# Two-layer diffusion trunk on one core: context products of gate and up made beside the sample products, activation sums kept in SBUF, modulation rows computed by halves

## The chip, the cores and the metric

One core of a Trainium2 chip runs the whole program. Its engines are TensorE (PE, with its weight loads as PEld), VectorE (DVE), ScalarE (ACT) and GpSimd (POOL); SyncE (SP) and POOL issue the DMAs that this text speaks of. The metric is the device time of one execution in microseconds (us), as the median of several runs.

## The reference

Two layers run over 256 context tokens and 1024 sample tokens (1280 columns in all, model width 1024, 8 blocks of 128). A layer has a modulated RMS norm, a projection into a pooling branch, a differential attention branch and a gating branch, an output projection, and a SwiGLU feed-forward part. The change lies in the second half:

```
m = silu(cond) @ w_ada + b_ada          -> sh1, sc1, g1, sh2, sc2, g2
x  = x + g1 * (y @ w_out)
h2 = rms_norm(x, norm2_g) * (1 + sc2) + sh2
gate, up = split(h2 @ w_ffn_in)         # 2 x 2816 columns
x  = x + g2 * ((silu(gate) * up) @ w_ffn_out)
```

The context and the sample use the same weights, with different conditioning vectors. D_FF = 2816 is 22 blocks of 128; the letter f counts them.

## The kernel before

Activations are held transposed (model width on the partitions, tokens along the free axis) in three chunks: c = 0 is the context (256 columns), c = 1 and c = 2 are the halves of the sample (512 columns each). All operands of matmuls are split into a rounded part and a remainder (`split`, L104: a copy on ACT at L105, a subtraction on DVE at L106), and each product takes three matmuls (`mm3`, L194, matmuls at L199). A weight slab is 128 x 1024 (512 KB): it is loaded by SP into a raw buffer and split into one of four buffers `w`.

The feed-forward input of a layer has two stages.

- The context stage: for each of the 22 f, the gate slab and the up slab are loaded and split, and two groups of 24 matmuls of 256 columns are made (`ctx_gate`, `ctx_up`). Into this loop are put the modulation of sample half c = 2 (`mod_keep`, f = 4 to 7) and, at f = 9, 11, 13 and 15, `act_sums`: four sums of activation blocks, made by POOL from modulated activations that had been written to DRAM (`HS`) and are read back into `q` (L1156), and then split.
- The sample stage: gate and up of both sample halves are a 2 x 2 block product. It is made with seven block products instead of eight (`seven`, products at L1200, each 12 matmuls of 512 columns), from sums of weight blocks (`sums`, POOL at L145 to L148) and the sums of activations. Both slabs of each f are loaded again here, into four raw buffers `raws` that take the place of the context activations. One call of `seven` for one f is called a seven below.

In layer 0, 64 rows of the modulation (`ada_row`, L246: a 128 x 1024 block of w_ada by SP into the raw ring of two, four multiply-and-reduce instructions on DVE at L255, each followed by the reading of its accumulator) are computed beside this: 8 during the output projection, and 56 during the seven products. The other 16 of layer 0 come earlier.

PE's order is the order in which the code is written. On the other engines a scheduler places the instructions when the program is built, as early as its own model of the buffers and the engines allows; each engine then runs its instructions in that order, and an instruction that waits holds up those behind it.

Of the kernel before, what the change touches and what calls it, by code (L numbers as in the profile page):

```python
# [38 lines left out]
SWAP = [(i + 16) % 32 for i in range(32)]  # L39

# [6 lines left out]
def build(tc, d):  # L47
# [45 lines left out]
    HS = [dr.tile([2, KD, P, 512], F32, name=f"HS{l}") for l in range(DEPTH)]  # L93
# [17 lines left out]
    def slab(src, extra=False):  # L111
        if extra:
            raw = pools["rx"].tile([P, 1024], F32, tag="rx", bufs=2, name=nm("raw"))
            nc.sync.dma_start(raw, src)
        else:
            raw = raw_slab(src)
        w = wp.tile([P, 2, 1024], F32R, tag="w", bufs=4, name=nm("w"))
        split(w[:, 0], w[:, 1], raw)
        ready.append(w)

    def sums(l, f):
        raws = []
        last = f == NF - 1

        def load(i):
            raw = wp.tile([P, 1024], F32, tag="raw", bufs=2, name=nm("raw")) if last else pools["raw"]()
            nc.sync.dma_start(raw, d["w_fi"][l, f, i])
            raws.append(raw)  # L130
            return raw

        def split_w(raw):
            w = wp.tile([P, 2, 1024], F32R, tag="w", bufs=4, name=nm("w"))
            split(w[:, 0], w[:, 1], raw)
            return w

        def second():
            u, g = load(1), raws[0]
            if last:  # L140
                wh = split_w(u)
            else:
                wh = pools["wh"].tile([P, 2, 512], F32R, tag="wh", bufs=2, name=nm("wh"))
                split(wh[:, 0], wh[:, 1], u[:, 512:])
# [4 lines left out]
            ready.append(wh if last else (split_w(g), wh))  # L149

        queue.extend([lambda: ready.append(split_w(load(0))), second])
        if last:
            queue.append(lambda: ready.append(split_w(raws[0])))
        queue.append(lambda: ready.append(split_w(raws[1])))

    def want(l):
        def add(src, *extra):
            queue.append(lambda: slab(src, *extra))
# [14 lines left out]
        for f in range(NF - 1):  # L173
            for i in range(2):
                add(d["w_fi"][l, f, i], f > 1 and f % 2 == 1)
        sums(l, NF - 1)
        for f in range(NF - 1):
            sums(l, f)
# [69 lines left out]
    def ada_row(l, j, condb):  # L248
        wt = raw_slab(d["w_adaT"][l, j])
# [19 lines left out]
    class Norm:  # L269
# [56 lines left out]
        def mod_keep(self, k, h, l, Ag, sh0, pair=True):  # L326
            q = COND[self.c]
            t = self.tmp()
            V.scalar_tensor_tensor(t, in0=self.x[:, k], scalar=Ag[l][:, k, q:q + 1], in1=self.rb,
                                   op0=ALU.mult, op1=ALU.mult)  # L330
            sh = mods[l][:, sh0 + k, q:q + 1]
            if pair:
                S.activation(h[:, 0, k], t, AF.Identity, bias=sh)
                V.scalar_tensor_tensor(h[:, 1, k], in0=t, scalar=sh, in1=h[:, 0, k].bitcast(F32),
                                       op0=ALU.add, op1=ALU.subtract)
            S.activation(self.x[:, k], t, AF.Identity, bias=sh)
# [179 lines left out]
    for l in range(DEPTH):  # L516
# [546 lines left out]
        prep = opened(pre, "pre")

        def spill(c):
            t0, n = CH[c]
            nc.gpsimd.dma_start(XS[:, t0:t0 + n].rearrange("(k p) t -> p k t", p=P), xs[c])

        for c in (1, 2):
            for m in range(4):  # L1070
# [3 lines left out]
                ada_next(1)  # L1074
        ws = load_w(4)
        ns = norms(prep, xs, 1)
        h2 = act_tiles("h2")

        def mod_c(c, k):
            ns[c].mod_keep(k, h2[c], l, A2, 3 * KD, c == 1 or k >= 4)  # L1080
            if k >= 4:
                nc.gpsimd.dma_start(HS[l][c - 1, k - 4::4].rearrange("k p t -> p k t"), xs[c][:, k - 4::4])

        order = [k for j in range(4) for k in (j, j + 4)]
        for c in range(3):
# [25 lines left out]
            spill(c)  # L1111
# [28 lines left out]
        tq = ExitStack()  # L1140
        tt = {}


        hq = ExitStack()

        def act_sums(j):
            if j == 0:
                pre.close()
                xq.close()
                for i in (3, 4):  # L1150
                    tt[i] = opened(tq, "tq", side="right").tile([P, 2, 4, 512], F32R, name=nm("T"))
                tt[2] = opened(fa, "t2").tile([P, 2, 4, 512], F32R, name=nm("T"))
                tt["q"] = opened(hq, "hq")
            q = tt["q"].tile([P, 2, 2, 512], F32, tag="q", bufs=1, name=nm("q"))
            for c in range(2):
                nc.sync.dma_start(q[:, c], HS[l][c, j::4].rearrange("k p t -> p k t"))  # L1156
            b11, b21, b12, b22 = q[:, 0, 0], q[:, 0, 1], q[:, 1, 0], q[:, 1, 1]
            G.tensor_sub(b11, b12, b11)
            G.tensor_sub(b12, b22, b12)
            G.tensor_sub(b22, b22, b11)  # L1160
            G.tensor_sub(b21, b21, b22)
            for t, src in ((h2[2], b11), (tt[3], b12), (tt[2], b22), (tt[4], b21)):
                split(t[:, 0, j], t[:, 1, j], src)
            if j == 3:
                hq.close()
                pools["wh"] = opened(fa, "wh")

        for f in range(NF):
            w = load_w(2)
            ctx_up(w[1], f, ctx_gate(w[0]))  # L1170
            if f == 2:
                ns[2].stat()
            if f == 4:
                ns[2].rows()
            if 4 <= f < 8:
                for k in order[2 * f - 8:2 * f - 6]:
                    mod_c(2, k)
            if 9 <= f < 16 and f % 2:
                act_sums((f - 9) // 2)
        raws = actp.tile([P, 4, 1024], F32, tag="act0", name=nm("raws"))  # L1180
        turn = [0]

        def next_raw():
            turn[0] += 1
            return raws[:, turn[0] % 4]

        pools["raw"] = next_raw
# [17 lines left out]
        t1, t2, t3, t4 = part(h2[2], 0), part(tt[2], 0), part(tt[3], 0), part(tt[4], 0)  # L1205
# [254 lines left out]
```

## Time and profile before

| | us |
|---|---|
| median of 3 runs | 3116.3 (3113.7 to 3119.6) |
| profiled execution, own time | 3117.8 |
| its span, first to last instruction | 3116.0 |
| layer 0: output projection, context stage, sample stage | 536 to 648, 648 to 800, 800 to 1281 |
| layer 1: context stage, sample stage | 2208.4 to 2359.8, 2359.8 to 2789.5 |

The stage times are from the span's start. In the span PE has matmuls under way for 2935.4 us, DVE is busy for 2046.8, ACT for 1170.7 and POOL for 619.2. In a group of instructions the first number after the bar is the time in which any of them ran, the second the mean length of one in ns, and behind the second bar stands the engine's idle time just before them, with what ended it.

### The profile page before, as it was taken

To read this page: it belongs to the slowest core of one execution; us is meant where nothing else is said; L and a number is where in the kernel's file an instruction comes from. 1 tells how busy PE (TensorE), PEld (TensorE's weight loads), DVE (VectorE), ACT (ScalarE), POOL (GpSimd) and SP (SyncE) were. 2 spreads that over 40 slices of the span, in tenths; PEclk is the share of its full clock that TensorE was granted. 3 is DMA by queue.
4 is the path that set the end of the run, shared out by engine and by line. 5 is a ranking of instruction groups with operands and counts; after the bars stand their busy time and mean duration, and the time that the engine had idled before them with its cause. 6 is when DMAs were issued, how large, how long until landed. Compare 5 with 4: busy or idle time off the path is not lost.

```text
span 3116.0 us, 41585 instructions
## 1 busy us (share of the span) xinstructions
PE 2935.4 (94%) x15800; PEld 2511.3 (81%) x15800; DVE 2046.8 (66%) x3221; ACT 1170.7 (38%) x1945; POOL 619.2 (20%) x703
## 2 busy tenths in 40 slices
PE   7999899998888899999989999999989999999997
PEld 5888788888776678888877887888888888888886
DVE  6876787676799954777684467873763444448777
ACT  4423676264222233311152236761643333322112
POOL 1222200023332333000021222000133333320002
PEclk9999999999999999999999999999999999999999
DMA  6576533366444431622123565331663222233221
GB/s 222 163 223 184 166 98 121 109 233 215 159 148 161 166 108 68 213 92 76 60 102 95 168 173 170 99 108 54 222 223 106 82 81 83 86 140 132 76 77 68
DMA packets 157815, 415.25 MB, mean 133 GB/s; under 512 B 19888, under 2 KB 51888, under 8 KB 157360
## 3 DMA queue, kind: packets, MB, share of 16 engines
q1 hardware_dynamic: 112608, 305.46, 30.4%
q0 software_dynamic: 44720, 106.98, 10.2%
q8 instruction: 124, 2.03, 0.3%
q14 instruction: 75, 0.61, 0.1%
q10 hardware_dynamic: 288, 0.16, 0.0%
HBM read 313.43 MB, written 99.09 MB: 132 GB/s over the span
## 4 chain that ended last, share of the span: by engine, by line
PE 66%; DVE 13%; DMA 8%; issue 6%; ACT 4%; POOL 2%; SPq 0%; DVEq 0%; POOLq 0%; ACTq 0%
PE f L199 26%; PE f L1200 19%; PE pa L199 7%; DVE ps L255 4%; PE pa L431 4%; PE S L371 4%; DMA raw<-w_adaT 4%; PE ps L389 3%; DVE w L106 2%; PE ps L904 2%; DMA kb<-KS 1%; DMA q<-HS 1%; DVE stt L375 1%; ACT E L378 1%; ACT w L105 1%
## 5 line engine op out<-in xcount | busy, mean ns | idle before, releaser
L199 PE MATMUL f<-ft,w 128*128 128x512 f32 (+1 forms) x3168 | 613.1, 356 | 0.7 <-DVE x L1027 0.7
L199 PEld LDWEIGHTS f<-ft,w 128*128 128x128 f32 x3168 | 523.1, 189 | 87.3 <-DVE x L1027 1.1
L1200 PE MATMUL f<-h,w 128*128 128x512 f32 x2112 | 505.8, 392 | 17.4 <-DVE pc L1230 9.4
L1027 DVE SCALAR_TENSOR_TENSOR x<-f,mod,x 128x512 f32<-128x512 f32 (+1 forms) x576 | 364.1, 658 | 221.9 <-PE f L199 220.7
L1200 PEld LDWEIGHTS f<-h,w 128*128 128x128 f32 x2112 | 396.6, 188 | 108.7 <-DVE pc L1230 14.8
L105 ACT CAST w<-raw 128x1024 fp32r<-128x1024 f32 x190 | 195.7, 1048 | 530.9 <-PE f L199 424.5
L106 DVE TENSOR_TENSOR w<-raw,w 128x1024 fp32r<-128x1024 f32 x190 | 233.8, 1245 | 113.1 <-ACT w L105 112.7
L199 PE MATMUL f<-h,w 128*128 128x256 f32 x2112 | 268.6, 291 | 34.0 <-DVE w L106 34.0
L199 PEld LDWEIGHTS f<-h,w 128*128 128x128 f32 x2112 | 265.2, 199 | 36.8 <-DVE w L106 36.7
L1200 PE MATMUL f<-T,w 128*128 128x512 f32 x1080 | 264.8, 394 | 2.3 <-ACT pc L1123 2.3
L199 PE MATMUL pa<-h,w 128*128 128x512 f32 (+1 forms) x1296 | 249.2, 353 | 0.8 <-DVE vn L607 0.8
L1200 PEld LDWEIGHTS f<-T,w 128*128 128x128 f32 x1080 | 203.8, 189 | 48.1 <-ACT pc L1123 2.7
L199 PEld LDWEIGHTS pa<-h,w 128*128 128x128 f32 x1296 | 212.3, 192 | 32.3 <-DVE vn L607 1.0
L375 DVE TENSOR_REDUCE stt<-S 128x1 f32<-128x1280 f32 x128 | 189.8, 1486 | 70.5 <-PE S L371 70.5
L431 PE MATMUL pa<-w,h 128*128 128x512 f32 x912 | 221.3, 401 | 9.5 <-DVE w L106 8.9
L199 PE MATMUL f<-mix,w 128*128 128x512 f32 (+1 forms) x1152 | 224.8, 355 | 0.0
L105 ACT CAST w<-raws 128x1024 fp32r<-128x1024 f32 x126 | 132.4, 1051 | 235.1 <-PE f L1200 196.2
L106 DVE TENSOR_TENSOR w<-raws,w 128x1024 fp32r<-128x1024 f32 x126 | 172.7, 1371 | 70.9 <-ACT w L105 70.9
L431 PEld LDWEIGHTS pa<-w,h 128*128 128x128 f32 x912 | 174.0, 193 | 50.6 <-DVE w L106 6.9
L199 PEld LDWEIGHTS f<-mix,w 128*128 128x128 f32 x1152 | 190.1, 189 | 29.5
L371 PE MATMUL S<-kb,aq 128*128 128x512 f32 (+1 forms) x768 | 196.7, 381 | 17.9 <-DMA kb<-KS 11.1
L1116 POOL DMA_DIRECT2D FS<-sg x132 | 72.6, 550 | 676.1 <-DVE sg L1232 511.0
(216 smaller groups left out, 3824.2 us busy)
## 6 DMA issues: line engine op xcount, KB each, us to landing
raw<-w_fi SPq DMA_DIRECT2D x88, 512.0 KB, 4.8
raws<-w_fi SPq DMA_DIRECT2D x84, 512.0 KB, 3.5
raw<-w_adaT SPq DMA_DIRECT2D x80, 512.0 KB, 3.9
ft<-FS SPq DMA_DIRECT2D x44, 640.0 KB, 5.1
FS<-sg POOLq DMA_DIRECT2D x88, 256.0 KB, 2.3
raw<-w_fo SPq DMA_DIRECT2D x44, 512.0 KB, 5.4
kb<-KS SPq DMA_DIRECT2D x64, 320.0 KB, 6.4
raw<-w_in SPq DMA_DIRECT2D x20, 512.0 KB, 3.8
```

Of the source, the lines that this page charges most:

```text
L105: S.copy(hi, src)
L106: V.tensor_sub(lo, src, hi.bitcast(F32))
L199: PE.matmul(ps, lhsT=a, rhs=b, start=(i == 0), stop=(i == n - 1))
L255: V.tensor_tensor_reduce(out=junk, in0=wt[:, u * 512:(u + 1) * 512], in1=condb[:, q, u * 512:(u + 1) * 512], scale=1.0, scalar=acc, op0=AL ...
L371: PE.matmul(ps[:, o:o + n], lhsT=aq[:, m, q0:q0 + P], rhs=kb[m][1 - p][:, o:o + n], start=(p == 0), stop=(p == 1))
L375: V.reduce_max(st[:, m:m + 1], ps[:, :nkey], axis=AX.X, negate=True)
L389: PE.matmul(o[:, :P], lhsT=pt[:, i * P:(i + 1) * P], rhs=vt(b + i), start=(b + i == 0), stop=(b + i == nk - 1))
L431: PE.matmul(ps, lhsT=a[:, y], rhs=wk[:, z], start=(k == 0 and x == 0), stop=(k == KD - 1 and x == 2))
L904: PE.transpose(T_["tp", b][:, x * P:(x + 1) * P], T_["E"][0][:, (4 * b + x) * P:(4 * b + x + 1) * P], ident)
L1027: V.scalar_tensor_tensor(xs[c][:, m], in0=ps, scalar=mods[l][:, g0 + m, COND[c]:COND[c] + 1], in1=xs[c][:, m], op0=ALU.mult, op1=ALU.add)
L1116: nc.gpsimd.dma_start(FS[l][f, :, t0:t0 + n], sg)
L1200: PE.matmul(ps, lhsT=y, rhs=z, start=(first and i == 0), stop=(i == 11), skip_group_check=not first)
```

## The change

- The context loop runs over f = 0 to 7 alone. For f = 8 to 21 the context's gate group is made inside `seven`, from the same split gate slab as the sample's, and the up group from the two split halves of the up slab (A21 and A22). For f = 0 to 6 both slabs are still loaded a second time; f = 7 is the first seven and uses the slabs of the last context step.
- `sums` makes the weight sums in another order with five POOL instructions for four, and splits A21 too (in every seven but the first). Raw slabs go round the ring of two and one further buffer `rx`.
- The sample activations live in four tiles `xg` (one for blocks k and k + 4 of both halves). They are modulated in place, `act_sums` reads them there, and its results T go into the same room; HS and q from DRAM are gone. `act_sums` runs at f = 2, 3, 4 and 5, right behind the modulation of c = 2.
- In the feed-forward part the modulation is computed by half rows (`ada_half`): 256 KB into two buffers `ra` of its own, two reductions each, with half of the conditioning vector in `condh`, which is loaded again when the other half begins. 8 rows belong to the output projection as before, 56 rows (112 halves) to the rest.
- The old `x` is written to XS in parts, and the squares for the norms go through two buffers.

```diff
+FIRST = 8
...
     def sums(l, f, i, first=False):
...
+                raws.append(wraw(d["w_fi"][l, f, 1], i + 1))
+                a22 = half(raws[1][:, 512:])
+            g, u = raws
             G.tensor_add(u[:, 512:], u[:, :512], u[:, 512:])
-            G.tensor_sub(u[:, :512], g[:, :512], u[:, :512])
             G.tensor_sub(g[:, :512], u[:, 512:], g[:, :512])
             G.tensor_sub(g[:, 512:], g[:, 512:], g[:, :512])
...
+            if first:
+                ready.append(split_w(g))
+            else:
+                ready.append(half(u[:, :512]))
+            G.tensor_sub(u[:, :512], u[:, 512:], u[:, :512])
+            G.tensor_sub(u[:, :512], u[:, :512], g[:, :512])
+            ready.append(split_w(u))
...
+    def ada_half(l, j, u, pool, first):
+        wt = pool.tile([P, 512], F32, tag="ra", bufs=2, name=nm("ra"))
+        nc.sync.dma_start(wt, d["w_adaT"][l, j, :, u * 512:(u + 1) * 512])
+        junk = psum()
+        for q in range(2):
+            o = mods[l][:, j, q:q + 1]
+            V.tensor_tensor_reduce(
+                out=junk, in0=wt, in1=pools["condh"][:, q], scale=1.0,
...
+        def mod_keep(self, k, l, Ag, sh0, h=None):
+            q, x = COND[self.c], self.x[:, k]
+            V.scalar_tensor_tensor(x, in0=x, scalar=Ag[l][:, k, q:q + 1], in1=self.rb, op0=ALU.mult, op1=ALU.mult)
+            S.activation(x, x, AF.Identity, bias=mods[l][:, sh0 + k, q:q + 1])
+            if h is not None:
+                split(h[:, 0, k], h[:, 1, k], x)
...
-            for c in range(2):
-                nc.sync.dma_start(q[:, c], HS[l][c, j::4].rearrange("k p t -> p k t"))
...
+            G.tensor_sub(q1, b12, b11)
+            G.tensor_sub(q3, b22, b12)
+            V.tensor_sub(q2, b22, q1)
+            G.tensor_sub(q4, b21, q2)
...
-        for f in range(NF):
+        for f in range(FIRST):
...
+            ada_halves(4 if f > 5 else 0)
+            if 2 <= f < 6:
+                for k in order[2 * f - 4:2 * f - 2]:
                     mod_c(2, k)
+                act_sums(f - 2)
...
+            if ctx:
+                pg = ctx_gate(wg)
+                ada_halves(2)
+            a21, s31 = (None, rest) if first else rest()
...
+            ada_halves(2)
+            if ctx:
+                ctx_up((a21, wh), f, pg)
```

On PE, in the sample stage, one seven stood alone. This is one of layer 0 before: f names the PSUM banks, h and T the activations, w and wh the split weights.

```order
L1200 MATMUL f_7757<-h_969_5414,w_7687 128x512 x12
L1200 MATMUL f_7692<-T_6622,w_7669 128x512 x12
L1200 MATMUL f_7784<-h_968_5413,w_7618 128x512 x12
L1200 MATMUL f_7692<-T_6614,w_7687 128x512 x12
L1200 MATMUL f_7828<-h_968_5413,w_7754 128x512 x12
L1200 MATMUL f_7692<-T_6618,wh_7662 128x512 x12
L1200 MATMUL f_7757<-h_969_5414,w_7669 128x512 x12
```

In the changed kernel PE's place from the middle of one seven with context to the middle of the next reads thus (L214 with h_987 are the context's matmuls of 256 columns).

```order
L1247 MATMUL f_7822<-h_988_5443,w_7819 128x512 x12
L1247 MATMUL f_7644<-T_6139,wh_7686 128x512 x3
L1247 MATMUL f_7644<-T_6222,wh_7686 128x512 x3
L1247 MATMUL f_7644<-T_6305,wh_7686 128x512 x3
L1247 MATMUL f_7644<-T_6388,wh_7686 128x512 x3
L214 MATMUL f_7862<-h_987_5442,wh_7782 128x256 x12
L214 MATMUL f_7862<-h_987_5442,wh_7686 128x256 x12
L1247 MATMUL f_7790<-h_989_5444,w_7692 128x512 x12
L1247 MATMUL f_7822<-T_6132,w_7899 128x512 x12
L1247 MATMUL f_7938<-h_988_5443,w_7819 128x512 x12
L214 MATMUL f_7954<-h_987_5442,w_7819 128x256 x24
L1247 MATMUL f_7997<-h_989_5444,w_7994 128x512 x12
```

The context's up group (from the halves wh_7782 and wh_7686) and its gate group (from the same w_7819 as the sample's) now stand between the seven products.

On DVE, in the context stage of layer 0, two context steps stood between one `act_sums` and the next: L106 is the remainder of a split, L1137 the product of gate and up.

```order
L106 TENSOR_TENSOR w_6643<-raw_6641,w_6643 128x1024
L1137 TENSOR_TENSOR sg_6603<-sg_6603,f_6578 128x256
L106 TENSOR_TENSOR w_6648<-raw_6646,w_6648 128x1024
L106 TENSOR_TENSOR w_6707<-raw_6705,w_6707 128x1024
L106 TENSOR_TENSOR h_969_5414<-q_6769,h_969_5414 128x512
L1137 TENSOR_TENSOR sg_6701<-sg_6701,f_6676 128x256
L106 TENSOR_TENSOR T_6614<-q_6769,T_6614 128x512
L106 TENSOR_TENSOR T_6622<-q_6769,T_6622 128x512
L106 TENSOR_TENSOR w_6712<-raw_6710,w_6712 128x1024
L106 TENSOR_TENSOR T_6618<-q_6769,T_6618 128x512
```

In the changed kernel DVE has in the same stage, for one step (L356 is the modulation, L1217 a sum, L1200 the product of gate and up):

```order
L356 SCALAR_TENSOR_TENSOR xg_4897<-xg_4897,A_0_87,ps_6116 128x512 x2
L106 TENSOR_TENSOR w_6233<-raw_6231,w_6233 128x1024
L106 TENSOR_TENSOR w_6238<-raw_6236,w_6238 128x1024
L1217 TENSOR_TENSOR q_6134<-xg_4897,q_6133 128x512
L106 TENSOR_TENSOR h_989_5444<-xg_4897,h_989_5444 128x512
L106 TENSOR_TENSOR h_989_5444<-q_6133,h_989_5444 128x512
L106 TENSOR_TENSOR T_6132<-q_6134,T_6132 128x512
L106 TENSOR_TENSOR T_6222<-q_6133,T_6222 128x512
L106 TENSOR_TENSOR T_6222<-q_6134,T_6222 128x512
L1200 TENSOR_TENSOR sg_6291<-sg_6291,f_6266 128x256
```

The modulation, all five small splits and one sum now stand together in each of four steps that follow each other, with two slab splits in the midst of them.

On DVE, in the sample stage of layer 0, a piece of a seven before (the ISA lines are a reduction and the reading of its accumulator):

```order
L1232 TENSOR_TENSOR sg_8087<-sg_8087,f_7971 128x512
L106 TENSOR_TENSOR wh_8220<-raws_7458,wh_8220 128x512
L255 ISA ps_8714,mod_84<-raw_8712,condb_5115,mod_84 128x512
L255 ISA mod_84 128x1
L1238 TENSOR_TENSOR sg_8149<-pc_8061,f_8036 128x512
L255 ISA ps_8721,mod_84<-raw_8719,condb_5115,cols 128x512
L255 ISA mod_84 128x1
L106 TENSOR_TENSOR w_8176<-raws_7458,w_8176 128x1024
L1240 TENSOR_TENSOR sg_8149<-sg_8149,pc_8105 128x512
```

And in the changed kernel:

```order
L1279 TENSOR_TENSOR pc_7065<-pc_7065,f_7040 128x512
L283 ISA ps_7676,mod_84<-ra_7674,condh_5303,cols 128x512
L283 ISA mod_84 128x1
L106 TENSOR_TENSOR w_7180<-raw_7112,w_7180 128x1024
L106 TENSOR_TENSOR wh_7257<-raw_7255,wh_7257 128x512
L283 ISA ps_7676,mod_84<-ra_7674,condh_5303,cols 128x512
L283 ISA mod_84 128x1
L283 ISA ps_7681,mod_84<-ra_7679,condh_5303,cols 128x512
L283 ISA mod_84 128x1
L283 ISA ps_7681,mod_84<-ra_7679,condh_5303,cols 128x512
L283 ISA mod_84 128x1
L1281 TENSOR_TENSOR sg_7029<-sg_7029,f_6929 128x512
```

Before, each of 13 sevens of layer 0 had 16 reductions but the last of them; now each of the first eight has 12 to 15 (mostly 14), each of the next five 20, all five with context products, and the last nine 2 in all. The splits of S31 (w_7180) and of the halves stand among them.

## Rows read from the trace of the kernel before

**Rows 1.** The page: busy time by engine, and the chain by engine.
```profile
PE 2935.4 (94%) x15800; PEld 2511.3 (81%) x15800; DVE 2046.8 (66%) x3221; ACT 1170.7 (38%) x1945; POOL 619.2 (20%) x703
PE 66%; DVE 13%; DMA 8%; issue 6%; ACT 4%; POOL 2%; SPq 0%; DVEq 0%; POOLq 0%; ACTq 0%
```

**Rows 2.** Table by stretch: busy us and count per engine, PE clock, DMA share, GB/s.
```profile
536.00:648.00 112.00, 112.00 (x594) 96.52 (x594) 76.73 (x173) 34.84 (x55) 12.50 (x13) 1.00 0.36 120
648.00:800.00 152.00, 134.82 (x1066) 133.61 (x1065) 95.58 (x112) 78.87 (x111) 47.00 (x50) 0.96 0.62 215
800.00:1281.00 481.00, 439.49 (x1851) 351.31 (x1851) 358.93 (x630) 144.06 (x198) 151.43 (x129) 0.98 0.41 137
849.48:1082.20 232.72, 205.19 (x840) 161.34 (x840) 215.98 (x413) 64.83 (x90) 74.75 (x60) 0.96 0.48 158
2208.40:2359.80 151.40, 134.54 (x1065) 133.12 (x1064) 97.85 (x112) 78.16 (x111) 47.16 (x51) 0.95 0.63 216
2359.80:2789.50 429.70, 425.75 (x1851) 348.06 (x1850) 176.58 (x199) 143.98 (x198) 140.12 (x129) 1.00 0.26 88
2402.60:2614.40 211.80, 211.80 (x926) 173.52 (x925) 86.19 (x99) 71.46 (x99) 71.83 (x66) 1.00 0.24 82
```

**Rows 3.** PE in order of time, context stage of layer 0: start, us, what.
```profile
683.49 34.79 PE L199 MATMUL f<-h,w 128*128 128x256 f32 x288
```

**Rows 4.** Groups on DVE from 2402.6 to 2614.4, layer 1: one of several.
```profile
L1224 DVE TENSOR_TENSOR sg<-pc,f 128x512 f32<-128x512 f32 x11 | 7.6, 687 | 55.1 <-PE f L1200 55.1
```

**Rows 5.** Groups on DVE from 849.48 to 1082.20, layer 0.
```profile
L255 DVE CUSTOM_DVE_ANT_0 ps<-raw,condb,cols 128x512 f32<-128x512 f32 x81 | 71.2, 888 | 16.0 <-DMA raw<-w_adaT 16.0
L106 DVE TENSOR_TENSOR w<-raws,w 128x1024 fp32r<-128x1024 f32 x30 | 46.3, 1544 | 0.0
L1224 DVE TENSOR_TENSOR sg<-pc,f 128x512 f32<-128x512 f32 x10 | 6.8, 683 | 0.0
```

**Rows 6.** DVE and POOL in order of time, inside one seven of layer 0.
```profile
1018.54 2.30 DVE L106 TENSOR_TENSOR w<-raws,w 128x1024 fp32r<-128x1024 f32 x1
1021.36 1.78 DVE L255 CUSTOM_DVE_ANT_0 ps<-raw,condb,mod 128x512 f32<-128x512 f32 x1
...
1024.78 0.75 DVE L255 CUSTOM_DVE_ANT_0 ps<-raw,condb,cols 128x512 f32<-128x512 f32 x1
...
1020.98 1.60 POOL L147 TENSOR_TENSOR raws<-raws 128x512 f32<-128x512 f32 x1 [1.23 <-DVE w L106]
```

**Rows 7.** Waits from 648 to 800: us in total, times, longest.
```profile
POOL q L1158 <- DMA q<-HS: 23.7, 4, 9.0
PE f L199 <- DVE w L106: 17.2, 6, 4.5
```

**Rows 8.** Groups on DVE and ACT from 648 to 800, context stage of layer 0.
```profile
L106 DVE TENSOR_TENSOR w<-raw,w 128x1024 fp32r<-128x1024 f32 x43 | 51.9, 1221 | 29.2 <-ACT w L105 29.2
L106 DVE TENSOR_TENSOR T<-q,T 128x512 fp32r<-128x512 f32 x12 | 13.9, 1165 | 0.7
L1137 DVE TENSOR_TENSOR sg<-sg,f 128x256 f32<-128x256 f32 x21 | 8.7, 415 | 5.2 <-PE f L199 5.0
L329 DVE SCALAR_TENSOR_TENSOR nt<-x,A,ps 128x512 f32<-128x512 f32 x12 | 8.7, 742 | 0.0
L105 ACT CAST w<-raw 128x1024 fp32r<-128x1024 f32 x43 | 44.2, 1042 | 25.9 <-PE f L199 11.4 <-DMA raw<-w_fi 6.7 <-POOL raw L148 5.2
L336 ACT ACTIVATE x<-nt,mod 128x512 f32<-128x512 f32 x14 | 9.9, 714 | 0.7 <-DVE nt L329 0.6
L105 ACT CAST T<-q 128x512 fp32r<-128x512 f32 x12 | 7.4, 620 | 9.9 <-POOL q L1160 4.3 <-POOL q L1159 3.5 <-POOL q L1161 1.9
```

**Rows 9.** DMA issues, KB each, median us to landing: 849 to 1082, and 648 to 800 (last).
```profile
raw<-w_adaT SPq DMA_DIRECT2D x40, 512.0 KB, 3.7
FS<-sg POOLq DMA_DIRECT2D x20, 256.0 KB, 2.7
raw<-w_fi SPq DMA_DIRECT2D x37, 512.0 KB, 5.0
```

More of the change, by code (lines that the diff above doesn't have):

```diff
@@ L109, in build, with wtile, wraw @@
     pools = {}
-    def slab(src, extra=False):
-        if extra:
-            raw = pools["rx"].tile([P, 1024], F32, tag="rx", bufs=2, name=nm("raw"))
-            nc.sync.dma_start(raw, src)
-        else:
-            raw = raw_slab(src)
-        w = wp.tile([P, 2, 1024], F32R, tag="w", bufs=4, name=nm("w"))
+    def wtile():
+        return wp.tile([P, 2, 1024], F32R, tag="w", bufs=4, name=nm("w"))
+    def wraw(src, i):
+        if i % 3 == 2 and "rx" in pools:
+            raw = pools["rx"].tile([P, 1024], F32, tag="rx", name=nm("raw"))
+            nc.sync.dma_start(raw, src)
+            return raw
+        return raw_slab(src)
@@ L118, in slab, with sums @@
+    def slab(src, i=0):
+        raw = wraw(src, i)
+        w = wtile()
         split(w[:, 0], w[:, 1], raw)
         ready.append(w)
-    def sums(l, f):
+        return raw
+    def sums(l, f, i, first=False):
         raws = []
[L125 to L131, printed above, removed]
@@ L133, in split_w, with half @@
         def split_w(raw):
-            w = wp.tile([P, 2, 1024], F32R, tag="w", bufs=4, name=nm("w"))
+            w = wtile()
             split(w[:, 0], w[:, 1], raw)
             return w
[L138 to L141, printed above, removed]
-            else:
-                wh = pools["wh"].tile([P, 2, 512], F32R, tag="wh", bufs=2, name=nm("wh"))
-                split(wh[:, 0], wh[:, 1], u[:, 512:])
+        def half(raw):
+            w = pools["wh"].tile([P, 2, 512], F32R, tag="wh", bufs=3, name=nm("wh"))
+            split(w[:, 0], w[:, 1], raw)
+            return w
@@ L148, in second, with rest @@
             G.tensor_sub(g[:, 512:], g[:, 512:], g[:, :512])
[L149 to L154, printed above, removed]
+            if not first:
+                ready.append((split_w(g), a22))
+        def rest():
+            g, u = raws
+            if first:
+                ready.append(split_w(g))
[4 more added lines that the diff above has]
+            ready.append(split_w(u))
@@ L156, in want, with add @@
+        queue.extend([gate, up, rest])
     def want(l):
-        def add(src, *extra):
-            queue.append(lambda: slab(src, *extra))
+        def add(src, *i):
+            queue.append(lambda: slab(src, *i))
         for j in range(4):
@@ L172, in want @@
             add(d["w_out"][l, m])
-        for f in range(NF - 1):
+        for f in range(FIRST - 1):
             for i in range(2):
[L175 to L178, printed above, removed]
+                add(d["w_fi"][l, f, i], 2 * f + i if f > 1 else 0)
+        sums(l, FIRST - 1, 2 * FIRST - 2, True)
+        for i, f in enumerate([*range(FIRST - 1), *range(FIRST, NF)]):
+            sums(l, f, 2 * (FIRST + i))
         for f in range(NF):
@@ L248, in ada_row @@
     def ada_row(l, j, condb):
[L249 removed]
+        raw = raw_slab(d["w_adaT"][l, j])
+        wt = [raw[:, :512], raw[:, 512:]]
         junk = psum()
@@ L1158, in act_sums @@
[L1158 to L1166, printed above, removed]
-        for f in range(NF):
+                tt["q"] = [pools["wh"].tile([P, 2, 512], F32, tag="wh", bufs=3, name=nm("q")) for _ in range(2)]
@@ L1210, in product1, with seven @@
             return wg, ps, copied(ps)
-        def seven(f, wg, pa_, p1, s24, wh, s31, more, first):
-            if not first:
-                fetch(1)
-            pc = fpsum(512)
-            product(pc, quarter(s31, 1), t1)
+        def seven(f, wg, pa_, p1, s24, wh, rest, more, ctx):
+            first = not callable(rest)
             product(pa_, quarter(s24, 0), t2, False)
```

154 lines of the change are left out of this document (87 added, 67 removed).

## The prediction

> **What bounds the kernel now.** I read the share of busy time first: TensorE (PE) is busy for 94 % of the span and carries 66 % of the chain, DVE 13 % and DMA 8 % [rows 1]. No matmul is removed by this change, so it can win only idle time of PE, and only in the stages that it touches. The table by stretch gives that. During the output projection (536 to 648) PE is busy for all 112.0 us, so nothing is lost there. The context stages take 152.0 us (layer 0) and 151.4 (layer 1), the sample stages 481.0 and 429.7 [rows 2], together 1214.1.
>
> What would PE alone need? In one unbroken run of the context stage 288 matmuls, 12 groups of 24, take 34.79 us [rows 3]: 2.90 a group, 5.80 for gate and up of one f, 127.6 for 22 f. In layer 1, 11 sevens take 211.80 us with PE busy throughout [rows 2]: 19.25 each, 423.6 for 22. The losses are then 24.4 and 23.8 in the context stages, 57.4 and 6.1 in the sample stages, 111.7 in all. That is the most the change can win.
>
> Who causes each? In the sevens of layer 1 DVE waits for PE (55.1 us over 11 sevens [rows 4]): PE is the bound. In layer 0 it is the other way: between 849.48 and 1082.20 ten sevens take 23.27 each, with DVE busy for 215.98 of 232.72 us [rows 2] and most of its remaining time waiting for the w_ada row (16.0 us [rows 5]). So a seven there lasts 21.60 of DVE work and 1.6 of waits. PE's granted clock is 0.96 there, near its upper level of 2.4 GHz, against 1.00 in layer 1 [rows 2]; that costs nothing of its own while PE waits. In the context stage PE waits 17.2 us for the remainders of slabs on DVE, and POOL 23.7 us for activations read back from DRAM [rows 7], with which the sums and their splits come late in DVE's order.
>
> **The context stage after.** The DRAM round trip and its 23.7 us go. What is late next is DVE itself, because modulation and sums of c = 2 now stand in four steps that follow each other. From the first modulation to the split that the first seven needs, DVE has 8 modulations of 0.74, 10 slab remainders of 1.22 [rows 8], 24 small remainders and subtractions of 0.68 (by the row of 0.683 for the same tile size [rows 5]) and 5 products of half that size, 0.42 by estimate: 5.9 + 12.2 + 16.3 + 2.1 = 36.5. Small remainders took 1.165 beside POOL before [rows 8]; 12 POOL operations now stand among them, and I stretch DVE by 0.69 for each: 8.2, in sum 44.7. In the same time PE has six f and half a group more, 6 x 5.80 + 2.7 = 37.5. So PE loses 7.2 in layer 1, and in layer 0, with 4 reductions more among them (2.7), 9.9. At the stage's start ACT's casts and modulations (1.042, 0.620 and 0.714 each [rows 8]) take about as long as PE's first groups; I charge 4 there and 2 for the first group itself. In layer 0 eight reductions and small splits stand behind the first S31 and before the next gate slab, some 9 us against the 5.5 that PE has at hand: 4. Sum: 20 in layer 0 and 13 in layer 1, each give or take 12.
>
> **Context with the sevens.** For 14 f in each layer the slabs are loaded once: 14 x 2 slab splits go in each layer, 28 x 1.22 = 34 us of DVE and 28 x 1.04 = 29 of ACT. PE's own work is the same 5.80 beside 19.25, so 25.05 for a seven with context. PE waited for little there in layer 1, and DVE has about 5 us to spare in each [rows 4]; the extra half split (0.68 on DVE, one POOL operation of 1.6) fits in. I charge 3 for layer 1's sevens.
>
> **Layer 0's sevens.** DVE's work has to be taken apart. Of the 21.60, 3 slab splits cost 3.66, six of 0.68 cost 4.1 and a stretch beside POOL some 3.1: a reduction takes 1.78 where POOL runs against 0.75 where it doesn't, a slab split 2.30 [rows 6] against 1.22. In ten sevens there are 30 such instructions, three to the four POOL sums. With 0.1 of others, 16 reductions are left at 0.665 each, their accumulator reads with them. After, each of the eight sevens without context has mostly 14 reductions, 3 slab splits, 7 small ones and five POOL sums: 9.31 + 3.66 + 4.76 + 4.12 = 21.85 (four stretches of 1.03), with 0.8 of waits 22.6. PE needs 19.25; the loss is 3.4, seven times (the first has its slabs): 23.8. Five sevens with context have 20 reductions and one more product: 13.30 + 3.66 + 4.76 + 0.42 + 4.12 = 26.26, with 1.4 of waits 27.7 against 25.05, so 2.6 x 5 = 13; of this I take off 6, as slabs lie split ahead by about one seven. The last nine have 2 reductions in all: no loss. Reloading the half conditioning vector in mid-sevens holds the reductions up once: 2.
>
> The waits for half rows are not shown by the trace. A whole row of 512 KB lands in 3.7 us, a 256 KB transfer on POOL's queue in 2.7 [rows 9], and the order leaves about 2 us between the release of a buffer and the reduction that wants it next, at some three places. So 0 to 3 us a seven, over 13 sevens from -12 to +24 around what I took; my value stands by the 2.7 row. The stretch is 3 to 5 a seven, another -14 to +12. In the output projection the eight rows are as many as before beside a PE that waits for nothing, and DVE is busy 76.73 of 112 us [rows 2]; cost 0, and 4 if the shorter transfers expose it.
>
> **A rule against this change.** In the trace a POOL sum of 1.60 lengthens a DVE instruction by about 1.03, three times in four, 0.77 per sum [rows 6]. The Trainium skill, "SBUF — State Buffer", section "Who interferes with whom", says that a DVE instruction with two SBUF inputs contends with a GpSimd instruction that reads SBUF, and that whoever issues second is blocked for the whole of it. By this rule the five sums would cost a seven 8.0 instead of 4.1; the trace bears it out only in part, so it stands below as a rival.
>
> **Sum.** Losses after: 20 + 13 + 23.8 + 7 + 2 + 3 = 68.8, against 111.7: a gain of 42.9. The profiled execution took 3117.8 (its span 3116.0, and 1.8 outside); 3117.8 - 42.9 = 3074.9. It lies 1.5 above the median of the runs, 3116.3; less that 3073.4, said as 3074.
>
> **The rivals.** *DVE's lag is not felt.* Slabs are split up to one seven ahead, and the last nine sevens have DVE nearly free, so PE might work off a reserve; the loss would be 30 (the two starts, and half of layer 0's first eight sevens), the time 3117.8 - 81.7 - 1.5 = 3035. For it: in layer 1 DVE waits for PE all along [rows 4]. Against: in layer 0 as it is, ten sevens in a row have no reserve [rows 5], and the new order still has eight in which DVE's work is above PE's. Chance 0.15.
>
> *The raw ring.* Three raw slots serve a seven where four did, and two of its sums work in place before the slots come free. A slab lands 5.0 us after its issue under load [rows 9]. If some 1.5 us of that shows in each seven, layer 1 loses 22 x 1.5 = 33 and the time is about 3107. For it: both slabs are read by POOL until late in the seven. Against: the order has each slab ready 6 us and more before it is wanted. Chance 0.12.
>
> *Slower: POOL and DVE exclude each other fully.* Each of the five sums then costs DVE its own 1.6: 8.0 - 4.1 = 3.9 more in each of 13 sevens of layer 0, 51; the 24 operations of the activation sums cost 0.91 more each where PE waits for DVE, 22. In layer 1's sevens DVE's spare time hides it. That makes 3074 + 73 = 3147. It turns from gain to loss where a POOL operation costs DVE 42.9 / 89 = 0.48 more than the 0.8 that I took, 1.3 us each. For it: the operations now stand close together, and there are more of them. Against: the measured 0.77. Chance 0.08. That the context products don't fit where they were put, and the second loads stay, is excluded by the order.
>
> **Chances and range.** My forecast has 0.65. Its own range is 3055 to 3095 (terms of ±12 in two stages, ±20 for waits and stretch, partly cancelling). The range for 8 in 10 reaches to both neighbours: 3040 to 3107. A change of 0.2 %, 6 us, is about what a measurement here can tell. Faster than that: the forecast, the first rival and the ring in most of its range, 0.84; the same 0.08, from the ring's upper end and a part of the exclusion; slower 0.08.
>
> **What would show it.** Per step: PE idle from the stage's start to the first seven's end 20 and 13 us, waiting for DVE's remainders, with no wait for DRAM left; the first eight sevens of layer 0 at 22 to 23 us and the five behind them at about 27, DVE busy throughout; the last nine and layer 1's at 25.05 with PE unbroken, 19.25 without context. I am wrong if PE waits in layer 1's sevens (the ring), if the first sevens of layer 0 come at 19 to 20 (the reserve), or if DVE's instructions beside POOL are all longer by 1.6 (exclusion).

## The result and the profile after

The changed kernel takes 3130.8 us (median of 8 runs, 3129.2 to 3148.1) against 3117.0 of the kernel before (8 runs): a ratio of 1.0055, 95 % interval 1.0038 to 1.0073. It is slower by half a percent. 3074 had been forecast, in a range of 3040 to 3107.

The page's busy time and chain of the changed kernel, beside [rows 1]:

```profile
PE 2940.2 (94%) x15800; PEld 2511.3 (80%) x15800; DVE 2034.7 (65%) x3215; ACT 1139.9 (36%) x1933; POOL 669.1 (21%) x737
PE 69%; DVE 13%; DMA 7%; issue 4%; ACT 4%; POOL 2%; SPq 0%; DVEq 0%; POOLq 0%; ACTq 0%
```

The page hardly shows a difference. The table by stretch does: layer 0's context stage, its eight sevens without context, the six sevens with context that have reductions, and the last eight; then layer 1's context stage and all its sevens (columns as in [rows 2]).

```profile
646.01:712.44 66.43, 52.04 (x394) 50.76 (x392) 60.63 (x77) 42.60 (x65) 29.54 (x22) 0.93 0.33 108
712.44:908.90 196.46, 167.82 (x673) 130.82 (x672) 178.91 (x300) 56.86 (x81) 75.21 (x60) 0.95 0.44 139
908.90:1094.50 185.60, 160.54 (x769) 132.37 (x770) 158.60 (x292) 42.36 (x66) 53.26 (x46) 0.95 0.42 133
1094.50:1299.75 205.25, 203.83 (x1083) 175.46 (x1082) 73.05 (x92) 62.82 (x89) 61.64 (x63) 1.00 0.25 84
2225.91:2293.08 67.17, 53.65 (x394) 52.45 (x393) 59.25 (x72) 42.45 (x65) 28.57 (x23) 0.90 0.33 106
2293.08:2800.25 507.17, 505.26 (x2523) 427.67 (x2523) 195.90 (x235) 164.86 (x235) 173.05 (x166) 1.00 0.23 78
```

With PE's prices (5.80 for an f of context, 19.25 for a seven) the losses are:

| stretch | before | forecast | after |
|---|---|---|---|
| layer 0, context stage | 24.4 (22 f) | 20 | 66.4 - 46.4 = 20.0 (8 f) |
| layer 0, sevens without context | | 23.8 | 196.5 - 8 x 19.25 = 42.4 |
| layer 0, sevens with context and reductions | | 7 + 2 | 185.6 - 6 x 25.05 + 2.9 = 38.2 |
| layer 0, last eight | | 0 | 1.9 |
| layer 0, all sevens | 57.4 | 32.8 | 82.5 |
| layer 1, context stage | 23.8 | 13 | 67.2 - 46.4 = 20.8 |
| layer 1, sevens | 6.1 | 3 | 2.4 |
| sum | 111.7 | 68.8 | 125.7 |

(The 2.9 is half an f of context: the first of those six makes the gate group alone, and the last of the 22 the odd up group.) PE loses 14.0 more than before; the medians lie 13.8 apart, the profiled executions 12.7 (3130.5 and 3117.8). Layer 1 wins 6.7, layer 0's context stage 4.4; layer 0's sevens lose 25.1 more, and every seven without context took 24.1 to 25.5 us there, where the kernel before took 23.27 [rows 2].

Where does a seven's time go? This is the stretch from 736.7 to 908.9, seven sevens without context (columns as above), with two of DVE's groups, and what PE and ACT wait for there (us in total, times, longest):

```profile
736.70:908.90 172.20, 146.36 (x589) 114.03 (x588) 157.60 (x264) 48.75 (x70) 62.55 (x50) 0.95 0.44 141
L283 DVE CUSTOM_DVE_ANT_0 ps<-ra,condh,cols 128x512 f32<-128x512 f32 x96 | 101.8, 1091 | 14.0 <-DMA ra<-w_adaT 13.4
L106 DVE TENSOR_TENSOR w<-raw,w 128x1024 fp32r<-128x1024 f32 x23 | 28.6, 1244 | 0.6 <-ACT w L105 0.6
```
```profile
ACT sg L1291 <- DVE sg L1290: 43.0, 7, 7.8
PE f L1247 <- ACT pc L1182: 23.2, 13, 2.5
```

PE waits for ACT's copy of a PSUM bank, ACT stands behind an activation that waits for DVE, and DVE is busy (157.6 us) or waiting (14.6, of which 13.4 for half rows) all the time. A reduction takes 1.091 in the mean; 0.753 where no POOL sum runs (third experiment). The time by which an instruction lasts longer than undisturbed is called a hold-up below. For the reductions it is 96 x 0.338 = 32.4 us; summed over all DVE instructions that took over 0.2 longer, it is 33.9, or 4.8 in a seven. Before, it was 3.2. The waits are 2.0 a seven, before 1.6 [rows 5].

One encounter of a POOL sum with reductions in order of time, and a sum that met no DVE instruction:

```profile
788.88 0.75 DVE L283 CUSTOM_DVE_ANT_0 ps<-ra,condh,cols 128x512 f32<-128x512 f32 x1
789.10 1.67 POOL L153 TENSOR_TENSOR raw<-raw 128x512 f32<-128x512 f32 x1 [11.15 <-DVE wh L106]
...
789.55 1.78 DVE L283 CUSTOM_DVE_ANT_0 ps<-ra,condh,cols 128x512 f32<-128x512 f32 x1
...
793.66 1.30 POOL L165 TENSOR_TENSOR raw<-raw 128x512 f32<-128x512 f32 x1
```

Alone the sum takes 1.30. At 789.10 it starts while a reduction is under way and takes 1.67; the next reduction takes 1.78, which is 1.03 over its own 0.75. Each holds the other up. Before, three of four sums met DVE in this way [rows 6]; now nearly all five do: in these seven sevens 34 DVE instructions are held up, beside 35 sums.

### The profile page after: what moved, and what is told of

Its sections match the earlier page's. It is cut to its first block, busy times and chain, and to the rows that moved or that the text cites. A ratio compares the mean times of both kernels' runs of the same rounds, so it can differ in the third digit from the quotient of the medians.

```text
span 3128.7 us, 41535 instructions
## 1 busy us (share of the span) xinstructions
PE 2940.2 (94%) x15800; PEld 2511.3 (80%) x15800; DVE 2034.7 (65%) x3215; ACT 1139.9 (36%) x1933; POOL 669.1 (21%) x737
## 4 chain that ended last, share of the span: by engine, by line
PE 69%; DVE 13%; DMA 7%; issue 4%; ACT 4%; POOL 2%; SPq 0%; DVEq 0%; POOLq 0%; ACTq 0%
PE f L214 29%; PE f L1247 18%; PE pa L214 7%; PE pa L454 4%; PE S L394 4%; PE ps L412 3%; DVE ps L283 3%; DMA ra<-w_adaT 3%; DVE w L106 2%; DMA kb<-KS 2%; PE ps L927 2%; DMA raw<-w_fi 1%; DVE stt L398 1%; ACT E L401 1%; ACT w L105 1%
## 5 line engine op out<-in xcount | busy, mean ns | idle before, releaser
L214 PE MATMUL f<-ft,w 128*128 128x512 f32 (+1 forms) x3168 | 613.8, 356 | 0.0
L214 PEld LDWEIGHTS f<-ft,w 128*128 128x128 f32 x3168 | 524.0, 190 | 86.4
L105 ACT CAST w<-raw 128x1024 fp32r<-128x1024 f32 x260 | 268.2, 1049 | 733.1 <-PE f L214 420.1
L1247 PE MATMUL f<-h,w 128*128 128x512 f32 x2112 | 513.3, 393 | 12.6 <-DVE w L106 8.1
L106 DVE TENSOR_TENSOR w<-raw,w 128x1024 fp32r<-128x1024 f32 x260 | 325.5, 1260 | 240.8 <-ACT w L105 240.7
L1247 PEld LDWEIGHTS f<-h,w 128*128 128x128 f32 x2112 | 395.6, 190 | 99.0 <-DVE w L106 9.2
L1067 DVE SCALAR_TENSOR_TENSOR x<-f,mod,x 128x512 f32<-128x512 f32 (+1 forms) x544 | 341.2, 654 | 169.1 <-PE f L214 166.3
L214 PE MATMUL pa<-h,w 128*128 128x512 f32 (+1 forms) x1296 | 249.5, 353 | 0.8 <-DVE vn L630 0.8
L214 PEld LDWEIGHTS pa<-h,w 128*128 128x128 f32 x1296 | 212.5, 192 | 32.3 <-DVE vn L630 1.0
L214 PE MATMUL f<-mix,w 128*128 128x512 f32 (+1 forms) x1152 | 224.8, 355 | 0.0
L313 POOL TENSOR_TENSOR nacc<-nacc,room 128x512 f32<-128x512 f32 (+1 forms) x45 | 52.0, 1155 | 771.7 <-ACT room L312 769.8
L214 PEld LDWEIGHTS f<-mix,w 128*128 128x128 f32 x1152 | 190.1, 189 | 29.5
L214 PE MATMUL f<-h,w 128*128 128x256 f32 x1440 | 189.9, 292 | 25.3 <-DVE w L106 25.3
L214 PEld LDWEIGHTS f<-h,w 128*128 128x128 f32 x1440 | 186.2, 200 | 29.7 <-DVE w L106 27.4
L401 ACT ACTIVATE E<-S,stt 128x1280 f32<-128x1280 f32 x128 | 170.4, 1331 | 39.1 <-DVE stt L398 39.0
```

Of the source, the lines that this page charges most:

```text
L105: S.copy(hi, src)
L106: V.tensor_sub(lo, src, hi.bitcast(F32))
L214: PE.matmul(ps, lhsT=a, rhs=b, start=(i == 0), stop=(i == n - 1))
L401: S.activation(E, ps[:, :nkey], AF.Exp, bias=st[:, m:m + 1], accum_out=st[:, 2 + m:3 + m])
L1067: V.scalar_tensor_tensor(xs[c][:, m], in0=ps, scalar=mods[l][:, g0 + m, COND[c]:COND[c] + 1], in1=xs[c][:, m], op0=ALU.mult, op1=ALU.add)
L1247: PE.matmul(ps, lhsT=y, rhs=z, start=(first and i == 0), stop=(i == 11), skip_group_check=not first)
```

## The experiments

Theory 1 was the forecast's own: a seven lasts as long as DVE's instructions in it, added up. Theory 2 was a fixed period, set by some chain. Theory 3 was formed after the first four runs: the build order fills DVE with as many reductions as its own timing has room for, so what that timing does not know (the hold-ups by POOL) is paid on top in every seven that has reductions.

**Reductions spread over all sevens, changed kernel.** The sevens' reductions are tied in DVE's order to a sum of their own seven, at all three places where a seven calls for them (one is shown; with context, the first place now takes three half rows instead of two):

```
-            V.tensor_add(g1, p1, pb)
+            at = V.tensor_add(g1, p1, pb)
...
-            ada_halves(2)
+            with tc.issue_after(at.ins):
+                ada_halves(2)
```

> The changed kernel, with each seven's reductions kept behind that seven's own sum on DVE, so that 6 stand in a seven without context and 12 in one with context, instead of 14 and 18 to 20 in the first fourteen and none in the last eight. Theory 1 (packing: a seven lasts as long as DVE's work in it, and DVE's spare time in the last eight is wasted): without context 25.0 less 8 reductions of 0.66 is 19.7, 0.5 over PE, in 8 sevens 4; with context 31.4 less 8 of 0.70 is 25.8, 0.8 over, in 14 sevens 11; the 80.8 us that layer 0's sevens lose become about 15, the time 3130.8 - 66 = 3065. Theory 2 (a fixed period of some 24.3 from the chain slab, half split, sum in place, split, since sevens with 12, 13 and 14 reductions all took 24.2 to 24.3): every seven with a reduction loses 5 to 6, now 22 of them, 120, the time 3170.

3074.8 us, ratio to the kernel before 0.9868 (0.9853 to 0.9883). Five sevens without context, with 6 reductions each:

```profile
781.20:877.40 96.20, 96.20 (x421) 78.85 (x420) 74.30 (x110) 35.55 (x51) 40.97 (x35) 1.00 0.37 125
L283 DVE CUSTOM_DVE_ANT_0 ps<-ra,condh,cols 128x512 f32<-128x512 f32 x30 | 32.7, 1118 | 5.3 <-DMA ra<-w_adaT 5.3
```

Each takes 19.24 with PE never idle, though the reductions are 1.12 long as before: a hold-up costs nothing where DVE has room. Theory 2 falls. Of the 10 us missing against 3065, most lie in the last seven, where the last reductions stand. It takes 34.34 where PE needs 25.05:

```profile
1213.88:1248.22 34.34, 27.57 (x134) 23.21 (x135) 18.70 (x31) 8.89 (x11) 5.28 (x7) 0.90 0.60 196
```

**The same in the kernel before**: its call behind a seven is put into such a block too.

> The kernel before, with the rows of each seven kept behind that seven's own sum on DVE in the same way: 8 or 12 reductions in every seven instead of 16 in the first thirteen. Theory 1: 23.2 less 4 or 8 of 0.665 is 20.5 or 17.9, so at most 1.3 over PE in every second seven and nothing where a reserve carries over; the losses of 4 in twelve sevens go, 3117 - 40 = 3077. Theory 2: nothing is won, 3117 to 3130. Against the first run it tells what the change is worth when neither kernel packs its rows.

3115.3, ratio 0.9991 (0.9979 to 1.0002): no gain. In layer 0's sevens there was one, 28 us (their losses sum to 29 instead of 57); twenty of them take 20.5 each. It was given back right behind them, in the second feed-forward product, where PE and ACT wait once for a transfer that stands behind the last rows:

```profile
822.90:1233.20 410.30, 392.99 (x1681) 313.09 (x1680) 302.53 (x585) 126.10 (x180) 123.33 (x118) 1.00 0.40 139
PE f L199 <- ACT ft L1272: 24.9, 1, 24.9
ACT ft L1272 <- DMA ft<-FS: 21.8, 6, 20.0
```

**The five weight sums on DVE, changed kernel.** In `sums` each `G.tensor_add` or `G.tensor_sub` becomes `V.`.

> The changed kernel, with the five sums of weight blocks on DVE instead of POOL. Theory 1 with exclusion (each POOL sum holds a DVE instruction up for 1.04, as the reductions' mean of 1.12 for 0.75 says): a sum costs DVE 0.68 instead of 1.04, 1.8 less per seven, in 14 sevens 25, the time 3106. Rival (the lengthening is not POOL's, the reductions are longer because of the half rows' arrival or their own form): DVE gets 3.4 more per seven, in 14 sevens 48, the time 3179.

3061.6, ratio 0.982 (0.9806 to 0.9835): 69 us below the changed kernel, where theory 1 had 25. Six sevens without context, their reductions, and one of the five sums on DVE:

```profile
762.90:878.40 115.50, 115.50 (x505) 94.63 (x504) 108.24 (x212) 43.19 (x61) 6.50 (x12) 1.00 0.47 155
```
```profile
L283 DVE CUSTOM_DVE_ANT_0 ps<-ra,condh,cols 128x512 f32<-128x512 f32 x61 | 45.5, 753 | 1.6 <-DMA ra<-w_adaT 1.1
L153 DVE TENSOR_TENSOR raw<-raw 128x512 f32<-128x512 f32 x6 | 4.1, 684 | 0.0
```

In these no loss is left; all of layer 0's sevens lose 10.5 instead of 82.5. The order took the five sums into account: it put 9 to 11 reductions into a seven instead of 14, and DVE's work is 18.0 a seven.

**No row loads**, changed kernel: one half row is loaded once and all reductions read it. The other loads are left out, so the modulation is not the reference's.

> The changed kernel, with one half row loaded once and read by all reductions of the feed-forward part: 127 loads of 256 KB are left out (the modulation that comes of it is not the reference's). If the waits for half rows (2.0 to 2.4 us in each of fourteen sevens) are paid in full, 30 less: 3101. If they only stand where DVE would wait for POOL or PE otherwise: 3125 to 3131.

3112.2, ratio 0.9978 (0.9968 to 0.9989): 19 us won, between the two. Four sevens:

```profile
763.20:860.50 97.30, 84.02 (x337) 65.96 (x337) 97.30 (x177) 28.32 (x43) 35.47 (x28) 0.95 0.19 65
```

DVE is busy for all 97.30 us, with no wait, and a seven still takes 24.3: the order now has 17 reductions in it for 14. The gain is that they end two sevens sooner. So the order had left room for the loads, and this run does not show how much of the waits for late rows is paid on top. With the third run it gave theory 3.

**The four weight sums on DVE, kernel before**: the same edit.

> The kernel before, with its four sums of weight blocks on DVE instead of POOL. Theory 3 (formed on the first runs: the build order fills DVE with as many reductions per seven as its own timing has room for, and that timing knows nothing of the time in which POOL's sums hold DVE up; so each sum on POOL adds its hold-up of about 1.04 to every seven that has reductions, whatever their number): the loss of 4 in twelve sevens goes, 57.4 becomes 10, the time 3118 - 47 = 3071. Theory 1 (DVE's work alone, added up): four sums cost DVE 2.7 instead of a hold-up of 3.1, 0.4 less in 13 sevens, 3113.

3062.5, ratio 0.9815 (0.9801 to 0.983). Theory 3 had 3071, theory 1 3113. Five sevens with 13 or 14 reductions lose nothing:

```profile
838.70:934.90 96.20, 96.20 (x421) 78.82 (x420) 94.45 (x198) 33.30 (x45) 5.42 (x10) 1.00 0.51 171
```

Layer 0's sevens lose 8.5 in all, for 57.4 before. It also tells what the change is worth without hold-ups in the sevens: 3061.6 against 3062.5, nothing that these runs can tell.

**Two of the five on DVE, changed kernel**: the two of `rest`.

> The changed kernel, with the last two of the five sums on DVE and three left on POOL. Theory 3: a seven with reductions loses 3 x 1.04 = 3.1 instead of 5.1 to 6, in 15 sevens 47 instead of 80.8, the time 3131 - 34 = 3097, between 3131 with five on POOL and 3062 with none. Theory 1: 2 x 0.36 less in 14 sevens, 10, 3121.

3093.4, ratio 0.9913 (0.9898 to 0.9928); theory 3 had 3097. Seven sevens without context took 20.6 to 23.6, in the mean 21.7:

```profile
735.20:887.30 152.10, 138.26 (x589) 109.14 (x588) 146.98 (x266) 49.23 (x71) 41.37 (x35) 1.00 0.46 152
```

**Activation sums on DVE too**: with the five weight sums on DVE, `G.` becomes `V.` for the three sums of `act_sums` that are on POOL.

> As the run with the five weight sums on DVE (3061.6), and the activation sums of the context stage on DVE too. If the losses of the context stage (21.0 and 20.4 there) are DVE's lateness, 12 hold-ups of 1.08 become 12 operations of 0.68, 5 less in each layer and no waits for POOL: 3052. If slab loads or ACT's casts set them: 3062, no change.

3045.2, ratio 0.9764 (0.9748 to 0.9781); 3052 was expected. The context stages, 46.4 each for PE, in the third run and then in this one:

```profile
651.97:719.34 67.37, 54.51 (x394) 53.52 (x393) 62.63 (x83) 43.67 (x66) 25.77 (x20) 0.88 0.33 112
2161.14:2227.91 66.77, 53.64 (x394) 52.50 (x392) 61.07 (x77) 43.83 (x67) 23.95 (x20) 0.90 0.32 109
648.60:710.80 62.20, 52.86 (x394) 51.56 (x393) 58.25 (x92) 43.61 (x66) 4.56 (x8) 0.92 0.35 117
2148.80:2209.80 61.00, 50.07 (x393) 48.68 (x392) 57.37 (x89) 43.46 (x66) 4.55 (x8) 0.97 0.35 119
```

They lose 15.8 and 14.6 instead of 21.0 and 20.4. That is 11 of the 16.4 us won; where the rest lies was not followed. DVE is still busy for 58 of 62 us: the stage is short of DVE itself.

**Context loop over 14 f, a step at every third**, weight sums on DVE:

```
-FIRST = 8
+FIRST = 14
...
-            if 2 <= f < 6:
+            if 2 <= f < 14 and f % 3 == 2:
```

> As the run with the five weight sums on DVE, and the context loop over f = 0 to 13 instead of 0 to 7, with a step of modulation and activation sums at every third f (2, 5, 8, 11) instead of four in a row. Six f more are loaded and split twice, 12 slab splits of 1.22 in each layer. If the context stage's loss is DVE's lateness: a step is 5.6 of DVE's own work and 3.2 of hold-ups, three f of slab splits and products 8.6, together 17.4 = three f of PE, so 5 to 8 of loss instead of 20 in each layer, and 3062 - 27 = 3035. If what the change won is the second loads, and not where the sums stand: 12 x 1.22 more in layer 0's sevens, 3062 to 3075.

3047.5, ratio 0.9771 (0.9755 to 0.9788); 3035 was expected. The context stages (PE needs 81.2), and the reductions in layer 0's:

```profile
648.08:748.98 100.90, 86.26 (x682) 85.27 (x680) 95.91 (x152) 57.48 (x84) 28.44 (x26) 0.95 0.53 177
2149.80:2238.20 88.40, 82.79 (x681) 81.73 (x680) 78.94 (x97) 58.13 (x85) 28.16 (x26) 1.00 0.49 164
L283 DVE CUSTOM_DVE_ANT_0 ps<-ra,condh,cols 128x512 f32<-128x512 f32 x28 | 23.8, 851 | 1.0 <-DMA ra<-w_adaT 1.0
```

Layer 1's stage lost 7.2, as expected. Layer 0's lost 19.7: the order had put 28 reductions into the longer stage, where the third run has 4.

**A sixth POOL operation, and a memset in its place**, changed kernel, at the end of `rest`:

```
+            if not first:
+                G.tensor_sub(g[:, 512:], u[:, 512:], g[:, :512])   # the other run: G.memset(g[:, 512:], 0.0)
```

> The changed kernel with a sixth POOL operation in each seven but the first: a difference of the same form (two inputs from SBUF) into room that nobody reads again, after the five sums. The reductions stand in the sevens as in the changed kernel. Theory 3: one more hold-up of about 1.04 in each of 13 sevens with reductions, 3131 + 14 = 3145; layer 1's sevens stay at 19.25. If POOL's operations cost nothing of their own: 3131.

> As the run with the sixth POOL operation, but it is a memset of the same room, which writes and reads nothing. If the hold-up comes of POOL's reading beside DVE's second input: 3131, as the changed kernel. If any POOL operation holds DVE up, or the later release of the slab does: 3136 to 3145.

3129.5 (ratio 1.0036, 1.0020 to 1.0053) and 3116.9 (1.0001, 0.9986 to 1.0015). Against the changed kernel both miss: the sixth sum costs nothing, and the memset wins 14. But adding an operation had changed DVE's order in some two hundred places, and with it hold-ups and waits. The two runs have one and the same order on PE, DVE, ACT and SP; against each other they differ by 12.6, where theory 3 has 14. POOL's operation and the reduction that stands beside it, with the sum and then with the memset:

```profile
811.19 1.72 POOL L168 TENSOR_TENSOR raw<-raw,raw 128x512 f32<-128x512 f32 x1 [3.06 <-DVE w L106]
```
```profile
811.87 1.59 DVE L285 CUSTOM_DVE_ANT_0 ps<-ra,condh,cols 128x512 f32<-128x512 f32 x1
```
```profile
807.36 0.52 POOL L168 MEMSET raw<- 128x512 f32 x1 [3.04 <-DVE w L106]
```
```profile
808.06 0.76 DVE L285 CUSTOM_DVE_ANT_0 ps<-ra,condh,cols 128x512 f32<-128x512 f32 x1
```

Three sevens at the same place in either:

```profile
791.20:864.30 73.10, 64.05 (x252) 50.03 (x252) 68.94 (x115) 20.70 (x30) 31.08 (x24) 0.93 0.43 141
```
```profile
787.60:857.50 69.90, 60.75 (x252) 48.13 (x253) 66.00 (x115) 20.69 (x30) 27.08 (x24) 0.98 0.45 148
```

24.37 a seven against 23.30, a difference of 1.07. DVE's busy time alone differs by 0.98 a seven, and the hold-ups (5.4 and 4.3) by 1.1. So the difference is the hold-up, and not the later release of the slab behind the longer operation, which would show as waiting.

**All sums on DVE with the wide context loop, and with reductions spread**:

> The context loop over f = 0 to 13 with a step of activation sums at every third f, and all sums, of weights and of activations, on DVE. From the run with the same loop and the activation sums on POOL (3047.5): its context stage lost 19.7 in layer 0, where the order puts 23 reductions more into it, and 7.2 in layer 1; without 12 hold-ups about 13 less in layer 0 and 3 in layer 1, 3032. If the stage is short of DVE itself: 3042.

> As that, with no reductions in the context loop and those of each seven kept behind that seven's own sum (10 in a seven without context, 12 in one with). Layer 0's context stage then loses as much as layer 1's, 4 to 7; the sevens have DVE work below PE's time throughout. 3028; if waits for half rows show in all 21 sevens instead of in 17, up to 3050.

3031.3 (ratio 0.9726, 0.9700 to 0.9751) and 3017.5 (0.9685, 0.9659 to 0.9712). Layer 0's context stage in the first (PE needs 81.2), and then, in the second, that stage, the sevens behind it and layer 1's stage:

```profile
646.30:747.50 101.20, 86.95 (x682) 85.97 (x681) 92.04 (x161) 57.62 (x84) 7.80 (x14) 0.93 0.54 176
```
```profile
655.20:739.20 84.00, 82.19 (x682) 81.61 (x681) 76.26 (x109) 57.90 (x86) 7.80 (x14) 1.00 0.53 180
739.20:1211.74 472.54, 470.75 (x2236) 392.95 (x2235) 397.05 (x784) 160.79 (x228) 28.86 (x53) 1.00 0.44 143
2137.50:2222.10 84.60, 82.12 (x681) 81.54 (x680) 75.99 (x109) 57.70 (x85) 7.79 (x14) 1.00 0.53 178
```

The first came out as expected (3032), but by luck: layer 0's stage loses 20.0, as much as with the activation sums on POOL (19.7), where 13 less had been expected. Layer 1's loses 3.3 instead of 7.2. What made up for it lies outside the feed-forward input and in the scatter of the run compared with (3040 to 3051).

With 161 DVE instructions in layer 0's stage 20 us are lost, with 109 it is 2.8, though the hold-ups are gone in both: packing alone costs that. The last kernel (3028 was expected) is faster than the kernel before by 3.2 % and than the changed one by 3.6 %.

## Why the prediction was wrong

**What bounds the kernel, and the most that can be won** held. PE had next to no idle time in layer 1's sevens (busy 505.3 of 507.2 us), DVE set layer 0's, and the sum of losses accounts for the result within 1.3 us (14.0 against 12.7 and 13.8).

**The context stage** came out as forecast in layer 0 (20) and 7.8 too low in layer 1. The step there charged 0.69 for each of 12 POOL operations; in the trace their hold-ups sum to 11.8 us instead of 8.2 in layer 1, and the run without them lost 5.7 less. The other 4 us of the miss were not followed. Layer 0's 20 was partly luck: the hold-ups are as large there (12.6), and the two stages lose about the same, though 6.7 had been charged for reductions in layer 0 alone.

**Layer 0's sevens is the step that failed**: 32.8 forecast, 82.5 measured. It took the number of reductions from the order and added up durations, with four hold-ups and 0.8 of waits. By size: hold-ups of 4.8 instead of 4.1 (nearly all five sums met DVE, not four) and waits of 2.0 instead of 0.8 in sevens without context, and eight of them losing for seven charged, 18.6; with context 31.4 instead of 27.7 (waits 3.3 for 1.4, DVE busy 28.1 for 26.3), a sixth such seven, and no reserve where 6 had been taken off, 29.2. The reserve could not build up, because every seven in front of those five ran late.

Behind these sizes is what the runs put in place of the sum. Take hold-ups and waits off a seven without context, and what is left is DVE's own work. It hardly changes with the edit:

| kernel | reductions | a seven | hold-ups | waits | left |
|---|---|---|---|---|---|
| before | 16 | 23.3 | 3.2 | 1.6 | 18.5 |
| changed | 14 | 24.6 | 4.8 | 2.0 | 17.8 |
| no row loads | 17 | 24.3 | 5.3 | 0 | 19.0 |
| two sums on DVE | 12 or 14 | 21.7 | 2.9 | 0.6 | 18.2 |
| sixth sum | 14 | 24.4 | 5.4 | 1.3 | 17.7 |
| memset | 14 | 23.3 | 4.3 | 1.1 | 17.9 |

(Hold-ups are summed over the records of DVE instructions that took over 0.2 longer than the same form takes undisturbed.) The rest lies between 17.7 and 19.0, under PE's 19.25; with the weight sums on DVE it is 18.0 and, in the kernel before, 18.9. So relieving DVE moves reductions forward and wins next to nothing per seven; what adds hold-ups is paid in full, in 14 sevens, as the sixth sum and the memset show. For the waits that is not shown: without row loads the order put in more reductions, and the seven stayed as long. The rest column was not forced to a value by any run; that the order plans for PE's length is inferred from it and from the number of reductions changing with the edits.

**The rule on POOL and DVE** had been put aside at a chance of 0.08, because a sum cost DVE 0.77 and not 1.6. In the lines above the sum is held up for 0.37 by the reduction under way, and the next reduction for 1.03 of the 1.22 that the sum still has. The trace agrees with the Trainium skill, "SBUF — State Buffer", section "Who interferes with whom": the second to issue is held for most of the time that the first still needs. Both prices were wrong: the record of 1.62 to 1.67 contains the sum's own wait for DVE, its work is 1.30, and a sum that meets DVE costs it about 1.0; 0.77 was a mean that counted the sums that missed DVE. At five sums that is 0.7 a seven more than I took, not 3.9. The memset, which reads nothing, held nothing up.

**The other rivals.** The lag was felt in every seven with reductions, so the first fell. The raw ring is no bound: layer 1's sevens lost 2.4 in 22. The slower side came from none of the three, but from the forecast's own mechanism at other sizes.

## What to carry to other kernels

Where a scheduler fills an engine up to the bound's period, do not price an edit by the work that it takes off that engine; ask what its timing does not see (here another engine's hold-ups), count that per period, and count the periods that are filled. Filler work with a distant due time belongs where the engine has spare time, tied there in the order, and must end before the next stage's loads. An operation given to a second engine may cost the first more than doing it itself: here 1.0 us of hold-up against 0.68.

## What was not expected of the hardware

PE's granted clock was 0.95 in the mean of layer 0's sevens in the changed kernel (736.7 to 908.9), where PE's waits are up to 2.5 us long. It was 1.00 in the same stage where the waits are gone (reductions spread, or sums on DVE), and also 1.00 in the run with two sums on DVE, with 14 us of idle time in 152; so idle time alone does not tell when the clock falls, and no run here tells more. A slower PE cost nothing extra there: DVE waited 14.0 us in front of its reductions and 0.6 for ACT, and never for PE.

A POOL memset of 128 x 512 took 0.52 and lengthened no reduction beside it, where a difference of two tiles of the same size took 1.72 and lengthened one by 0.83 (1.59 for 0.76).
